# An encoder block in one kernel: the p products moved into the routing, h kept as two tensors, the last down products and the gate in halves

## The chip, the cores and the metric

The kernel runs on one core of a Trainium2 chip. The metric is the device time of one execution in microseconds, lower is better; a state of the kernel is timed in several runs and the median is compared. Times in the text are microseconds (us). The engines are named as in the profile: PE (TensorE, matmul), DVE (VectorE), ACT (ScalarE), POOL (GpSimd) and SP (SyncE, which here only issues transfers).

## What is computed

One layer of an encoder over 1024 tokens of width 1024, all in float32. What matters for the change is the second half of the layer:

```python
h = h + merged @ w_out                                     # residual after the token mixers
xn = rmsnorm(h, norm_ffn)
aff = softmax(xn @ w_router)                               # 1024 x 16
top_aff, top_idx = top_k(aff.T, 128)                       # each expert takes 128 tokens
xg = xn[top_idx]                                           # 16 x 128 x 1024
hid = silu(xg @ w_gate) * (xg @ w_up)                      # 16 experts, 1024 x 1024 each
y = (hid @ w_down) * top_aff
h = h + zeros.at[top_idx].add(y)
ple_gate = sigmoid(rmsnorm(h, norm_ple) @ w_pg)            # 1024 x 1024
h = h + ple_gate * (p @ w_ple)                             # p: 1024 x 256, w_ple: 256 x 1024
out = rmsnorm(h, norm_final)
```

## The kernel before

**Matmuls.** Every float32 product is made of three: each operand is split into a rounded high part and the rest (`split`, a CAST on ACT and a subtraction on DVE), and `mm3` (L124 for its matmuls) multiplies high by high, high by low and low by high into one bank of PSUM. Transposes are `turn` (L127). While `in_order` is set, PE runs `mm3` and `turn` in the order in which the program calls them; the other engines' order is the scheduler's, bent by `issue_after`, and the order of an engine is fixed when the program is built.

**Tile loop** (about 875 to 996 us). `w_half(t, c, between)` makes column half c of merged @ w_out for token tile t, and calls steps of the tile before at set places within its matmuls (`h_turned`, `router`, `affinities`, `aff_turned`). Its result is added into `ht` by DVE (L1194), and POOL writes `ht` to `h_d` in memory. `aff_turned` copies the turned affinities into `cand` (L1249, L1251), and after tiles 3, 5 and 6 a part of the selection's sorting follows on DVE (`four_tiles`, `two_tiles`, `merged`; MAX8 and MATCH_REPLACE, L1076 and L1078).

**Routing** (996 to 1020). After the last tile DVE finishes the sort, finds each expert's threshold (`cg`), and masks and matmuls with `tri` and `ones` give each token its place; `tokens(e)` turns places into indices by one-hot matmuls (L1345), `gather(e)` fetches the rows (`xg`) by an indirect DMA on POOL. Between these steps stand eight of the sixteen halves of p @ w_ple, `p_half(0)` to `p_half(7)`: 6 matmuls of 128x512 each, whose result ACT scales (L1173) into a slot and writes to `pw_d` in memory.

**Experts** (1020 to 1591). Each expert is 12 quarters (4 each of gate, up, down) of 1 MB of weights: `quarter_of` loads it by SP (the pieces 12 to 15 by POOL) into one of 15 buffers named by `cycle`, splits it into high and low parts (slots of `whl`, every third of `rawE`), and makes 12 matmuls of 128x512. `begin` turns an expert's rows, `hidden_turned` its hidden values; `down(e - 1)` follows `up(e)`. The down result is scaled by ACT (L1458) and added into `h_d` by one indirect scatter of 4 KB rows per expert.

**Gate** (1591 to the end). The other half of the p products (tiles 4 to 7, eight halves, in `p_product`) is made first, with the loads of p and w_ple for them; then `front(t)` turns a tile's rows of h and sums their squares, and `ple(t)` makes the gate's product with w_pg (whose rows are scaled by a gain when it is split, L982), the sigmoid by Tanh, the sum and the last norm.

## Time and profile before

| | us |
|---|---|
| median of 3 runs | 1713.43 (1713.2 to 1713.58) |
| profiled execution | 1716.04 |
| its span, first to last instruction | 1714.3 |
| PE busy | 1640.6 (96%) |
| DVE busy | 1172.4 (68%) |
| ACT busy | 904.7 (53%) |
| POOL busy | 155.4 (9%) |
| mean granted clock of PE, as a share of 2.4 GHz | 0.986 |

PE is busy nearly always, so the rows to look for are those in which it waits, and those in which its matmuls take longer than elsewhere at a lower granted clock (the two levels are 1.2 and 2.4 GHz; 0.50 in a stretch means that all of it was at the lower one). A timeline row that ends in brackets gives the idle time of the engine ahead of the row, and the instruction whose end released it.

### The profile page before, as it was taken

The numbers are of one execution on the slowest core, as the hardware profiler recorded it, in microseconds if no ns is written. First come the engines' busy times: TensorE is split into PE (matmuls) and PEld (weight loads), VectorE is DVE, ScalarE is ACT, GpSimd is POOL, SyncE is SP. The second block draws the span as 40 slices with busy tenths as digits, with TensorE's granted clock in tenths as the row PEclk, the third lists the DMA queues.
The fourth block names the chain that finished last, engine by engine and source line by source line (L and its number), as shares of the span: only waits on it lengthen the run. The fifth ranks groups of instructions, "written<-read, shape, count | busy, mean of one in ns | idle before, by whom it ended". The sixth has DMA issues, their size and how long they took to land. (4 is left out here: it accounts for less than half of the span.)

```text
span 1714.3 us, 23072 instructions
## 1 busy us (share of the span) xinstructions
PE 1640.6 (96%) x8795; PEld 1347.7 (79%) x8795; DVE 1172.4 (68%) x2228; ACT 904.7 (53%) x1273; POOL 155.4 (9%) x186
## 2 busy tenths in 40 slices
PE   7999989998999999999999959999999999999897
PEld 7978856567889898988887647888888887777786
DVE  7446655553474747473356878999999998888666
ACT  5345545542443435352033237777777777777632
POOL 1013300000000000000001110111111111100010
PEclk9999999999999999999999979999999999999999
DMA  6033421225121121126452589999999999992811
GB/s 234 2 106 123 136 61 50 62 98 173 50 65 59 56 69 43 44 75 234 147 198 111 193 333 375 382 397 388 394 391 398 394 387 370 377 380 88 275 50 50
DMA packets 123607, 335.06 MB, mean 195 GB/s; under 512 B 9180, under 2 KB 41988, under 8 KB 123496
## 3 DMA queue, kind: packets, MB, share of 16 engines
q1 hardware_dynamic: 106784, 277.96, 44.4%
q0 software_dynamic: 14704, 53.17, 9.1%
q10 hardware_dynamic: 2008, 2.46, 0.4%
q8 instruction: 69, 1.13, 0.3%
q14 instruction: 42, 0.34, 0.1%
HBM read 290.50 MB, written 43.06 MB: 195 GB/s over the span
## 5 line engine op out<-in xcount | busy, mean ns | idle before, releaser
L131 DVE TENSOR_TENSOR slot<-slot 128x2048 fp32r<-128x2048 f32 (+1 forms) x200 | 446.5, 2246 | 52.5 <-ACT slot L131 50.0
L131 ACT CAST slot<-slot 128x2048 fp32r<-128x2048 f32 (+1 forms) x200 | 374.8, 1879 | 104.2 <-PE ps_mm L124 57.0
L124 PE MATMUL ps_mm<-aT_h,wh 128*128 128x512 f32 x512 | 204.8, 400 | 0.0
L124 PE MATMUL ps_mm<-aT_l,wh 128*128 128x512 f32 x512 | 201.4, 393 | 0.0
L124 PE MATMUL ps_mm<-aT_h,wl 128*128 128x512 f32 x512 | 200.8, 392 | 0.0
L124 PE MATMUL ps_mm<-slot,xt_h 128*128 128x512 f32 x512 | 161.7, 396 | 3.1 <-DVE slot L131 2.7
L124 PE MATMUL ps_b<-slot,xt_h 128*128 128x512 f32 x512 | 160.2, 393 | 4.0 <-DVE slot L131 4.0
L124 PE MATMUL ps_mm<-slot 128*128 128x512 f32 x576 | 140.5, 398 | 0.0
L124 PEld LDWEIGHTS ps_mm<-slot 128*128 128x128 f32 x576 | 106.7, 189 | 24.2 <-issue 1.4
L124 PEld LDWEIGHTS ps_mm<-slot,xt_h 128*128 128x128 f32 x512 | 96.0, 190 | 23.7 <-DVE slot L131 3.5
L124 PEld LDWEIGHTS ps_b<-slot,xt_h 128*128 128x128 f32 x512 | 95.1, 188 | 24.7 <-DVE slot L131 5.7
L124 PEld LDWEIGHTS ps_mm<-aT_h,wh 128*128 128x128 f32 x512 | 96.6, 189 | 22.6 <-issue 6.2
L124 PEld LDWEIGHTS ps_mm<-aT_h,wl 128*128 128x128 f32 x512 | 96.6, 189 | 18.6
L124 PEld LDWEIGHTS ps_mm<-aT_l,wh 128*128 128x128 f32 x512 | 96.7, 189 | 16.4
L131 DVE TENSOR_TENSOR wl<-raw,wh 128x2048 fp32r<-128x2048 f32 (+1 forms) x29 | 60.9, 2105 | 60.9 <-ACT wh L131 60.9
L124 PE MATMUL ps_mm<-slot,xt_l 128*128 128x512 f32 x256 | 100.6, 393 | 0.6 <-DVE xt_l L131 0.6
L124 PE MATMUL ps_b<-slot,xt_l 128*128 128x512 f32 x256 | 99.8, 390 | 0.0
L131 ACT CAST wh<-raw 128x2048 fp32r<-128x2048 f32 (+1 forms) x30 | 51.9, 1734 | 82.0 <-PE ps_mm L124 78.2
L124 PE MATMUL ps_mm<-wh,aT_h 128*128 128x256 f32 x320 | 90.5, 283 | 0.0
L124 PE MATMUL ps_mm<-wl,aT_h 128*128 128x256 f32 x320 | 89.5, 280 | 0.0
L124 PE MATMUL ps_mm<-wh,aT_l 128*128 128x256 f32 x320 | 89.2, 279 | 0.0
L124 PE MATMUL ps_mm<-slot,nT_h 128*128 128x512 f32 (+1 forms) x272 | 81.9, 382 | 0.4 <-ACT nT_h L131 0.4
(386 smaller groups left out, 3281.8 us busy)
## 6 DMA issues: line engine op xcount, KB each, us to landing
slot<-in_w_exp_gate_dram SPq DMA_DIRECT2D x64, 1024.0 KB, 7.8
slot<-in_w_exp_down_dram SPq DMA_DIRECT2D x64, 1024.0 KB, 8.4
slot<-in_w_exp_up_dram SPq DMA_DIRECT2D x60, 1024.0 KB, 7.9
raw<-in_w_in_dram SPq DMA_DIRECT2D x16, 1024.0 KB, 6.6
raw<-in_w_in_dram SPq DMA_DIRECT2D x14, 512.0 KB, 5.2
sg_d<-sgr POOLq DMA_DIRECT2D x14, 512.0 KB, 2.9
xn_d<-xa POOLq DMA_DIRECT2D x8, 520.5 KB, 3.3
xt<-in_x_dram SPq DMA_DIRECT2D x8, 512.0 KB, 6.8
```

What stands on the lines that cost most here:

```text
L124: return on_pe(nc.tensor.matmul(*args, **kw))
L131: return nc.scalar.copy(hi, src), eng.tensor_sub(lo, src, hi)
```

## The change

Seven things are changed together.

1. All sixteen halves of p @ w_ple are made within the last tile's routing: one ahead of `h_turned(7)`, then one behind it, one behind the router, two behind the affinities, six behind `aff_turned`, one behind the turns of `cg`, two behind the `ones` matmuls, and two behind `tokens(0)`, whose own matmuls now stand in PE's program order. Both loads of p and the one of w_ple come at tile 3, the turns of p at tiles 4 and 5. The results of halves 8 to 15 stay in slots of `rawE` until they are written to `pw_d`.
2. `aff_turned(7)` makes its four copies on DVE (two were on ACT).
3. `four_tiles()` is called in the second half product of tile 4, behind its add, not behind `aff_turned(3)`.
4. `h_d` is two tensors, for the low and the high 512 columns, and each expert's result goes out in two scatters of 2 KB rows.
5. The down products of experts 13, 14 and 15 are made by column halves (`down_half`): the low half of 13 between gate and up of expert 15, then low 14, low 15, high 13, high 14, high 15. From expert 14 on the ring of weight buffers is 10 long.
6. w_pg is loaded into free buffers ahead of its split, and the low-half rows of tiles 0 to 3 are fetched while the high halves run.
7. The gate of tiles 0 to 2 starts with the inner blocks 0 to 3 (the low columns of h) of all three, in six banks; then the high columns are turned and the rest follows.

```diff
-    h_d = dram.tile([T, D], F32, name="h_d")
+    h_d = [dram.tile([T, 512], F32, name=x) for x in ("h_lo", "h_hi")]
...
         for g in range(2):
-            pt = bank("tr")
+            pt = bank("b")
...
+            with tc.issue_after(made):
+                four_tiles()
+        nc.gpsimd.dma_start(h_d[c][tt], ht[:, cc])
         if c == 1:
-            nc.gpsimd.dma_start(h_d[tt], ht)
             ss = small.tile([128, 1], F32, name="ss")
             junk = o2.tile([128, D], BF16, name="junk", bufs=1)
...
             to, by = cand[t][(group[t] + q) * 32:(group[t] + q) * 32 + NE], pa[0:NE, q * n:q * n + n]
-            if q % 2 and t == NT - 1:
-                nc.vector.tensor_copy(to, by)
+            if t == NT - 1:
+                placed = nc.vector.tensor_copy(to, by).ins
...
-        if t == 3:
-            four_tiles()
-        elif t == 5:
+        if t == 5:
             two_tiles()
         elif t == 6:
             merged(top[0:NE], one_tile(6), slice(0, NE), top)
...
-            p_raw = p_load(slot(rawX, (2, 4, 256))[:, 0], 0)
+        if t == 3:
+            p_raw = slot(rawX, (2, 4, 256))
+            for i in range(2):
+                p_load(p_raw[:, i], 4 * i)
             wp = parts(loaded(rawX, (2, D), w_ple), (2, D), (rawC, rawC))
-        if t == 5:
-            pT = slot(rawC, (2, 4, 2, 128), F32R)
-            p_turned(p_raw, pT)
+        elif t in (4, 5):
+            pTs.append(slot(rawC, (2, 4, 2, 128), F32R))
+            p_turned(p_raw[:, t - 4], pTs[-1])
 
 
     def p_half(n):
         nonlocal pw
         i, c = n // 2, n % 2
         if n % 4 == 0:
-            pw = slot(rawX, (2, D))
-        p_product(pw, pT, wp, i, (c,))
+            pw = slot(rawX if n < 8 else rawE, (2, D))
+        cc = slice(c * 512, c * 512 + 512)
+        pT = pTs[i // 4]
+        po = bank("mm" if c else "b")
+        for k in range(2):
+            mm3(po, pT[:, 0, i % 4, k], pT[:, 1, i % 4, k], wp[0][:, k, cc], wp[1][:, k, cc], k == 0, k == 1)
+        nc.scalar.mul(pw[:, i % 2, cc], po, 0.5)
         if n % 4 == 3:
             nc.scalar.dma_start(pw_d[(i - 1) * 128:(i + 1) * 128].rearrange("(c p) n -> p c n", p=128), pw)
 
     pw = None
     p_half(0)
-    for f, more in ((h_turned, (1,)), (router, (2,)), (affinities, (3, 4)), (aff_turned, (5, 6, 7))):
+    for f, more in ((h_turned, (1,)), (router, (2,)), (affinities, (3, 4)), (aff_turned, range(5, 11))):
         f(NT - 1)
         for n in more:
             p_half(n)
...
+    p_half(11)
     thr = o1.tile([128, 2, NE], F32, name="thr")
     nc.vector.tensor_copy(thr, pt[:, 0:2 * NE].rearrange("p (i e) -> p i e", i=2))
...
     pr = pr[:, 0:256].rearrange("p (a t e) -> p a t e", a=2, t=NT)
     sl0 = o1.tile([128, NT, NE], F32, name="sl0")
...
-            nc.tensor.matmul(pi[:, 0:2], oh[:, t], tok[:, t], start=t == 0, stop=t == NT - 1)
+            (nc.tensor.matmul if e else matmul)(pi[:, 0:2], oh[:, t], tok[:, t], start=t == 0, stop=t == NT - 1)
...
-
+    p_half(14)
+    p_half(15)
...
+    def scatter(e, c):
+        nc.gpsimd.indirect_dma_start(out=h_d[c][:, :], in_=st[e]["y"][:, c * 512:c * 512 + 512], in_offset=None,
+                                     compute_op=ALU.add,
+                                     out_offset=bass.IndirectOffsetOnAxis(ap=st[e]["idx"][:, 0:1], axis=0))
+
+    def down_half(e, c, po, after=()):
+
+        s = st[e]
+        cc = slice(c * 512, c * 512 + 512)
+        for k2 in range(2):
+            n = n_pieces[0]
+            raw = loaded(next_pool(), (4, 512), w_ed[e][k2 * 512:k2 * 512 + 512, cc])
+            hi, lo = [slot(rawE if n % 3 == 2 else whl, (4, 512), F32R) for _ in range(2)]
+            split(hi, lo, raw)
+            for k in range(4):
+                kk = 4 * k2 + k
+                mm3(po, s["hT"][0][:, kk], s["hT"][1][:, kk], hi[:, k], lo[:, k], kk == 0, kk == KC - 1)
+            for f in after if k2 == 0 else ():
+                f()
+        nc.scalar.mul(s["y"][:, cc], po, s["col"][:, e:e + 1])
+        scatter(e, c)
+
     def hidden_turned(e):
...
-        last = {1: partial(hidden_turned, e)} if e == NE - 1 else {}
         gate(e, {1: partial(hidden_turned, e - 1)} if e else {0: first_tokens})
-        up(e, {1: partial(tokens_of, e + 2)} if e else {2: partial(ahead, 1)})
-        if e:
-            down(e - 1, {0: partial(ahead, e + 1), **last})
-    down(NE - 1, {})
-
-    in_order[0] = False
-
-
...
-    cycle, n_pieces = [rawC] * 4 + [rawX] * 2 + [wraw] * 2 + [rawE] * 2 + [rawB] * 2 + [rawD], [0]
-    pws = {}
-    p_raw = p_load(next_slot((2, 4, 256))[:, 0], 4)
-    wp = parts(loaded(next_pool(), (2, D), w_ple), (2, D), (next_pool(), next_pool()))
-    pT = next_slot((2, 4, 2, 128), F32R)
-    p_turned(p_raw, pT)
-    wg = {(k, 0): mpiece(w_pg, 4 * k, 0, next_pool(), LL, gain=plcol) for k in range(2)}
-    for i in range(4):
-        if i % 2 == 0:
-            pw = next_slot((2, D))
-        p_product(pw, pT, wp, i)
-        pws[4 + i] = pw[:, i % 2]
...
+        if e == NE - 2:
+            cycle = [rawA] * 3 + [rawX] * 2 + [wraw] * 2 + [rawB] * 2 + [rawA]
+        if e == NE - 1:
+            st[NE - 3]["y"] = e2.tile([128, D], F32, name="y")
+            down_half(NE - 3, 0, bank("a"))
+        up(e, {1: partial(tokens_of, e + 2), 2: partial(ahead, NE - 1 if e == NE - 2 else NE)} if e else
+           {2: partial(ahead, 1)})
+        if 0 < e < NE - 2:
+            down(e - 1, {0: partial(ahead, e + 1)})
...
+    def first_turn(t):
+        nT = slot(whl, (2, KC, 128), F32R)
+        nTs[t] = nT[:, 0], nT[:, 1]
+        return turned_half(hs_[t], nTs[t], 0)
...
+    for c in range(2):
+        for i, e in enumerate(ends):
+            if c or i:
+                down_half(e, c, bank("b" if i % 2 else "mm"),
+                          (partial(hidden_turned, NE - 1), first_rows) if c == 0 and i == 1 else ())
+        if c == 0:
+
+            for t, rp in ((0, rawD), (2, rawC)):
+                r = lo_rows[t] = rp.tile([128, 2, D], F32, tag="raw", name="raw")
+                hs_.update({t: r[:, 0], t + 1: r[:, 1]})
+    wg, pws = {}, {}
+    raws = {}
+    for k in range(2):
+        for c in range(2):
+            raws[k, c] = loaded(rawX if k else rawC, (4, 512), w_pg[k * 512:k * 512 + 512, c * 512:c * 512 + 512])
+
+    def gate_parts(k):
+        for c in range(2):
+            pl = AA if c else (wraw if k else rawB,) * 2
+            wg[k, c] = mpiece(w_pg, 4 * k, 512 * c, None, pl, gain=plcol, raw=raws[k, c])
+
+    gate_parts(0)
+    with tc.issue_after(last_load[0]):
+        for t in (0, 2):
+            rows(lo_rows[t], h_d, t, (0,))
+        for t in range(3):
+            here = first_turn(t)
+        with ExitStack() as es:
+            for i in here:
+                es.enter_context(tc.issue_after(i.ins))
+            gate_parts(1)
+        sE.close()
+        f2 = ctx.enter_context(pool("f2", bufs=2, side="right"))
+        nfin = slot(whl, (2, D))[:, 0]
+        nc.sync.dma_start(nfin, bcast_row(norm_final, D))
+        for t in (0, 2):
+            rows(lo_rows[t], h_d, t, (1,))
+        for t in range(0, NT, 2):
+            if t > 3:
+                r = rawC.tile([128, 2, D], F32, tag="raw", name="raw")
+                rows(r, h_d, t)
+                hs_.update({t: r[:, 0], t + 1: r[:, 1]})
+            r = slot(rawX if t < 3 else rawE, (2, D))
+            nc.sync.dma_start(r, pw_d[t * 128:(t + 2) * 128].rearrange("(c p) n -> p c n", p=128))
+            pws.update({t: r[:, 0], t + 1: r[:, 1]})
+    F = {}
...
+        if t not in nTs:
+            nTs[t] = hl_pair(f2, "nT")
+            turned_half(ht, nTs[t], 0)
+        here = turned_half(ht, nTs[t], 1)[0].ins
...
+        with tc.issue_after(here):
+            nc.scalar.activation(junk, ht, AF.Square, accum_out=ss)
...
-    front(0)
-    front(1)
+    begun = {}
+    for t, tag in enumerate(("b", "mm", "a")):
+        begun[t] = [bank(tag) for _ in range(2)]
+        for po, (c0, n) in zip(begun[t], columns(t)):
+            product(po, t, c0, n, range(4))
+    for t in range(3):
+        front(t)
     for t in range(NT):
-        if t + 2 < NT:
+        ple(t, begun.get(t))
+        if t < 2:
+            front(t + 3)
+        elif 2 < t < NT - 2:
             front(t + 2)
-        ple(t)
```

**PE in the routing.** Of before, from the last turn of affinities (`affA`) to the first `tri` matmul; rows of 128x512 into `ps_b` are p products (six to a half):

```order
L127 MATMUL ps_a<-ident,affA 16x128
L124 MATMUL ps_b<-slot 128x512 x18
L127 MATMUL ps_a<-ident,cg 128x16 x2
L124 LDWEIGHTS tri
L124 MATMUL ps_a<-msk,tri 128x256
```

Of after, the same place:

```order
L127 MATMUL ps_a<-ident,affA 16x128
L124 MATMUL ps_mm<-slot 128x512 x6
L124 MATMUL ps_b<-slot 128x512 x6
L124 MATMUL ps_mm<-slot 128x512 x6
L124 MATMUL ps_b<-slot 128x512 x6
L124 MATMUL ps_mm<-slot 128x512 x6
L124 MATMUL ps_b<-slot 128x512 x6
L127 MATMUL ps_a<-ident,cg 128x16 x2
L124 MATMUL ps_mm<-slot 128x512 x6
L124 LDWEIGHTS tri
L124 MATMUL ps_a<-msk,tri 128x256
```

Six halves stand between the turn of `affA` and that of `cg` where three were, and one more ahead of `tri`.

**DVE at tile 4.** Of before, from the last affinities of tile 3 (`affA`) over the sort's last step to the second half's add (`ht`) of tile 4:

```order
L1238 TENSOR_SCALAR affA<-affA,rd_8992 128x16
L1076 MAX part<-cand_8470 128x8 x2
L1078 MATCH_REPLACE cand_8470<-part,cand_8470 128x64 x2
...
L1076 MAX part<-cand_8470 128x8 x2
L1194 SCALAR_TENSOR_TENSOR ht<-ps_mm,ht 128x512
L1100 TENSOR_TENSOR b_8475<-part 128x64
```

Of after:

```order
L1234 TENSOR_SCALAR affA<-affA,rd_8999 128x16
L1187 SCALAR_TENSOR_TENSOR ht<-ps_mm,ht 128x512
L1077 MAX part<-cand_8471 128x8 x2
L1079 MATCH_REPLACE cand_8471<-part,cand_8471 128x64 x2
...
L1077 MAX part<-cand_8471 128x8 x2
L144 TENSOR_SCALAR rs_v_9113<-ss 128x1
L131 TENSOR_TENSOR slot<-ps_b,slot 128x512
```

The add of `ht` now precedes the list of MAX and MATCH_REPLACE.

**ACT at the end.** Of before, from the last y (the down product's result) on; `slot<-ps_b` of L1173 are p products, `slot<-slot,cols` of L982 is the split of w_pg, and the CAST of `ps_tr` the first turned rows:

```order
L1458 ACTIVATE y<-ps_b,col 128x512 x2
L131 CAST slot<-ps_tr 128x512 x2
L1173 ACTIVATE slot<-ps_b 128x512 x3
L982 ACTIVATE slot<-slot,cols 128x512 x8
L1173 ACTIVATE slot<-ps_b 128x512 x4
L1547 ACTIVATE junk,ssf<-raw 128x1024
L1173 ACTIVATE slot<-ps_b 128x512
L131 CAST nT_h<-ps_tr 128x512 x2
```

Of after, the column halves of y being named `xg` and `hid` for the tiles that they reuse, and the split of w_pg L983:

```order
L1472 ACTIVATE xg<-ps_b,col 128x512
L983 ACTIVATE slot<-slot,cols 128x512 x5
L1472 ACTIVATE hid<-ps_mm,col 128x512
L983 ACTIVATE slot<-slot,cols 128x512 x3
L131 CAST slot<-ps_tr 128x512 x3
L983 ACTIVATE slot<-slot,cols 128x512 x8
L131 CAST slot<-ps_tr 128x512
L1611 ACTIVATE junk,ssf<-raw 128x1024
```

The p multiplies are gone, and five and three multiplies of w_pg stand ahead of the CAST of the first turned rows, with the last y between them.

## Rows read from the trace of the kernel before

**Rows 1.** The page, parts 1 (busy us, share, instructions) and 5 (busy us, mean ns).

```profile
PE 1640.6 (96%) x8795; PEld 1347.7 (79%) x8795; DVE 1172.4 (68%) x2228; ACT 904.7 (53%) x1273; POOL 155.4 (9%) x186
...
L131 DVE TENSOR_TENSOR slot<-slot 128x2048 fp32r<-128x2048 f32 (+1 forms) x200 | 446.5, 2246 | 52.5 <-ACT slot L131 50.0
```

**Rows 2.** Stretches: window, length, busy us by engine, PE clock, DMA share, GB/s.

```profile
1010.00:1020.00 10.00, 0.64 (x10) 0.59 (x11) 7.60 (x8) 0.00 (x0) 4.99 (x4) 0.50 0.46 157
1020.00:1030.00 10.00, 10.00 (x49) 7.78 (x48) 6.52 (x6) 3.41 (x5) 1.96 (x2) 0.70 1.02 408
1060.00:1500.00 440.00, 436.55 (x2108) 360.33 (x2107) 400.83 (x251) 341.09 (x264) 59.76 (x25) 1.00 1.02 387
```

**Rows 3.** Timeline of PE, tile 4: start, length, instruction, [idle before <- releaser].

```profile
943.14 0.66 PE L127 MATMUL ps_tr<-ident,ht 128*128 128x128 f32 x4 [2.68 <-DVE ht L1194]
943.55 3.76 PE L124 MATMUL ps_mm<-slot 128*128 128x512 f32 x9
```

**Rows 4.** Timeline of DVE, the same stretch.

```profile
937.58 0.35 DVE L1076 MAX8 part<-cand 128x8 f32<-128x64 f32 x2 [2.87 <-ACT cand L1251]
...
942.41 0.67 DVE L1194 SCALAR_TENSOR_TENSOR ht<-ps_mm,ht 128x512 f32<-128x512 f32 x1
```

**Rows 5.** Timeline of PE in the routing behind the last tile.

```profile
996.16 4.38 PE L124 MATMUL ps_b<-slot 128*128 128x512 f32 x18
1006.66 0.26 PE L127 MATMUL ps_a<-ident,cg 16*128 16x16 f32 x1 [6.12 <-DVE cg L1306]
...
1008.38 0.37 PE L124 MATMUL ps_a<-msk,tri 128*128 128x256 bf16 x1 [0.91 <-DVE msk L1318]
...
1012.00 0.38 PE L1345 MATMUL ps_a<-tok,oh 128*128 128x2 bf16 x8 [2.50 <-DVE oh L1341]
1019.74 1.94 PE L127 MATMUL ps_a<-ident,xg 128*128 128x128 f32 x8 [7.36 <-DMA xg<-xn_d,idxs]
```

**Rows 6.** Timeline of DVE, start of the last tile's sort.

```profile
996.94 0.18 DVE L1249 COPY cand<-ps_a 16x32 f32<-16x32 f32 x1 [0.29 <-ACT cand L1251]
998.67 0.18 DVE L1249 COPY cand<-ps_a 16x32 f32<-16x32 f32 x1 [1.55 <-ACT cand L1251]
```

**Rows 7.** Waits of PE, 1420 to 1592: us, times, longest us.

```profile
PE ps_b L124 <- DVE slot L131: 3.4, 3, 1.3
PE ps_mm L124 <- DVE slot L131: 2.7, 2, 1.3
PE ps_b L124 <- DVE hT_l L131: 0.8, 1, 0.8
PE ps_b L124 <- ACT hT_h L131: 0.4, 1, 0.4
```

**Rows 8.** Timeline of PE behind the last down product.

```profile
1591.43 1.03 PE L127 MATMUL ps_tr<-ident,slot 128*128 128x128 f32 x8
1592.85 7.18 PE L124 MATMUL ps_b<-slot 128*128 128x512 f32 x30 [0.38 <-ACT slot L131]
1603.36 5.72 PE L124 MATMUL ps_b<-slot 128*128 128x512 f32 x18 [3.34 <-ACT slot L1173]
...
1610.40 0.73 PE L124 MATMUL ps_mm<-slot,nT_h 128*128 128x512 f32 x2 [0.44 <-ACT nT_h L131]
```

**Rows 9.** Timeline of ACT, the same stretch.

```profile
1597.84 5.00 ACT L982 ACTIVATE slot<-slot,cols 128x512 fp32r<-128x512 f32 x8
```

**Rows 10.** Transfers: 1100 to 1400 (two rows).

```profile
DMA packets 30774, 118.36 MB, mean 395 GB/s; under 512 B 1938, under 2 KB 1938, under 8 KB 30757
...
q0 software_dynamic: 2448, 8.99, 11.0%
```

**Rows 11.** Waits of SP's queue, 1100 to 1400.

```profile
SPq L971 <- DVE slot L131: 235.5, 95, 3.2
```

**Rows 12.** Loads issued 960 to 1060: KB, median us to landing.

```profile
slot<-in_w_exp_up_dram POOLq DMA_DIRECT2D x4, 1024.0 KB, 10.1
```

**Rows 13.** Scatters: the last one; then all traffic of h_d, to landing.

```profile
h_d<-y,idxs POOLq DMA_INDIRECT x1, 6.4
...
DMA to landing us min/median/max: 2.8/10.4/13.6
```

More of the change, by code (lines that the diff above doesn't have):

```diff
@@ L1508, in tile_hybrid_block @@
-    hs_ = {}
-    def rows(src, t, n=2):
-        r = next_pool().tile([128, 2, D], F32, tag="raw", name="raw")
-        return r, nc.sync.dma_start(r[:, 0:n], src[t * 128:(t + n) * 128].rearrange("(c p) n -> p c n", p=128)).ins
-    def keep(d, t, n, r):
-        d.update({t + i: r[:, i] for i in range(n)})
-    r, first = rows(h_d, 0, 1)
-    keep(hs_, 0, 1, r)
-    with tc.issue_after(first):
-        wg.update({(k, 1): mpiece(w_pg, 4 * k, 512, next_pool(), AA, gain=plcol) for k in range(2)})
-        keep(pws, 0, 2, rows(pw_d, 0)[0])
-        keep(hs_, 1, 2, rows(h_d, 1)[0])
-        nfin = next_pool().tile([128, 2, D], F32, tag="raw", name="raw")[:, 0]
-        nc.sync.dma_start(nfin, bcast_row(norm_final, D))
-        for t in (2, 4, 6):
-            keep(hs_, t + 1, 2 if t < 6 else 1, rows(h_d, t + 1, 2 if t < 6 else 1)[0])
-            if t == 2:
-                keep(pws, t, 2, rows(pw_d, t)[0])
@@ new lines, in rows, with first_rows @@
+    def rows(r, src, t, halves=range(2)):
+        for c in halves:
+            nc.sync.dma_start(r[:, :, c * 512:c * 512 + 512],
+                              src[c][t * 128:(t + 2) * 128].rearrange("(c p) n -> p c n", p=128))
+    ends = range(NE - 3, NE)
+    hs_, nTs = {}, {}
+    def first_rows():
+        st[NE - 1]["y"] = e2.tile([128, D], F32, name="hid")
+    def first_turn(t):
+        nT = slot(whl, (2, KC, 128), F32R)
+        nTs[t] = nT[:, 0], nT[:, 1]
+        return turned_half(hs_[t], nTs[t], 0)
@@ L1572, in ple @@
         sm = small.tile([128, 1], F32, name="ssm")
[L1573 removed]
+        nc.vector.tensor_reduce(sm, ss[:, 0:len(columns(t))], axis=X, op=ALU.add)
         rs = rstd_of(sm, D)
```

81 lines of the change are left out of this document (39 added, 42 removed).

## The prediction

> **What bounds the kernel now.** I read the engine totals first: TensorE is busy for 1640.6 us of a span of 1714.3 [rows 1], so a gain must take matmul time off the path, fill an idle stretch, or raise the clock in one. Next the stretches [rows 2]: in the 440 us of the experts PE is busy for 436.6 at a clock of 1.00, so almost nothing is to be had there. In 1010 to 1020 (routing's end) it is busy for 0.64 us of 10 at a clock of 0.50. Then I went through PE's and DVE's rows where the diff touches them: the sorting beside tile 4 [rows 3, 4], the routing tail [rows 5, 6], the late experts [rows 7] and the stretch between the last expert and the first gate product [rows 8, 9]; last, what the DMA queues have in hand [rows 10 to 13].
>
> The profiled execution took 1716.04 us with a span of 1714.3; the median of three is 1713.43. I sum changes against the span and subtract the sum from the median, as though the launch costs the same.
>
> **The p products leave the end.** Between the end of the last down product (1591.43) and the first gate product (1610.40) lie 18.97 us [rows 8]: 8 turns of p (1.03), 48 matmuls of eight halves (7.18 + 5.72), waits of 0.38, 3.34 and 0.44, and the first front's turns. The 48 cost 0.239 us each in the first row (7.18/30) and 0.318 in the second (5.72/18), so the second ran partly at half clock after the 3.34 us of idle: 18 at the first rate would be 4.3. All of this goes; the p products' work moves into gaps of the routing (below). In its place, PE turns four blocks for each of tiles 0 to 2 and waits for ACT and DVE. ACT's new order puts the last y product's multiply, which waits for the last matmul, ahead of three gate multiplies and the CAST of the turned rows. An ACT operation on 128x512 takes 5.00/8 = 0.63 us [rows 9]; four multiplies and the CAST, 3.1 us, then a DVE subtraction of the same size, 3.7, and two or three hand-overs of 0.38 as in [rows 8]: 4.5 us. 18.97 less 4.5 is 14.5 gained. Against it I set 0.4 for a hand-over at the second half turns of tiles 0 to 2, which now stand in a row ahead of the rest of the gate, and 1.0 for a lower clock after the new idle (the 18 matmuls above lost 1.4 after 3.34 us of it). The 72 matmuls on low column halves (72 x 0.239 = 17.2 us) cover the last high-half scatter and its rows: multiply 0.6, scatter and landing 6.4 to 10.4 [rows 13], and for 0.5 MB pieces of rows about half of the 10.1 us of 1 MB [rows 12]; 12 to 16 us. **End: -13.1, bounds -17 (nothing lost in clock or hand-overs, turned rows ready at once) to -9 (the rows late, or a dip as long as the one at 1603).**
>
> **Routing.** Eight halves in place of those that ran there before (halves 1 to 7, and one turn of p is in the tile loop already) come into the gaps. What is on the path is DVE's: the copy of the second candidates waited 1.55 us for ACT's, which stood behind p multiplies, so the sort began behind it, after 998.85, where the matmuls behind the affinities' turn had begun at 996.16 [rows 5, 6]. All four copies on DVE remove that wait and the 0.29 ahead of the first, and add two copies of 0.18: -1.5. In PE's order half 11 now precedes the tri matmul: the gap there is 0.91 us [rows 5], the half 1.46 (6 x 4.38/18): +0.55. Halves 12 and 13 precede the one-hot matmuls, whose gap is 2.50 [rows 5]; two halves cost 2.9: +0.3 to +0.4. Halves 14 and 15 follow those matmuls, where PE waits 7.36 us for the gathered rows: hidden. So the gather starts about 0.8 earlier. Halves 5 to 10 (8.8 us) replace 18 matmuls (4.38) and fill most of the 6.12 us wait for cg: 4.4 us more against 6.1, hidden with 1.7 to spare, at full clock.
>
> **The experts' start** has a gain and a loss. PE ran at half clock there: the granted clock is 0.50 for 1010 to 1020 and 0.70 for 1020 to 1030 [rows 2]. With p halves in the gaps I expect the clock to be held to about 1014 and the idle before the gather to be some 4 to 5 us, not 7; of the 3 us that a clock of 0.70 costs in those 10 I count somewhat under half as saved: -1.3. The loss: the third quarter's hi and lo parts go to slots of rawE, which hold p rows 8 to 15 until these are written out. They are multiplied last (half 15 at about 1014), and 1 MB transfers among the expert loads there took 10.1 us to land [rows 12], so the last is out about 1025 to 1027; DVE's subtraction for that quarter (2246 ns in the mean [rows 1]) starts then and the next quarter's stands behind it. PE would want that quarter about 1026 and gets it about 1029. Some of this is met by the pieces behind it being prepared at 2.25 against some 2.8 for PE's 12 matmuls (0.239 each [rows 8]): +2.8 less 0.5. Net with the earlier gather (-0.8) and clock (-1.3) it is about **+0.2, and with the copies' reserve not all turned into time I take +0.5; bounds -2.5 (dip gone, p rows out early) to +4.5 (dip kept, p rows 3 us later).**
>
> **The tile loop.** The sort of four tiles (4.83 us of DVE, 937.58 to 942.41) stood ahead of tile 4's second residual add, and PE waited 2.68 us for it, then ran 9 matmuls in 3.76 us where the rate of [rows 8] makes 2.2 of them [rows 3, 4]. The change puts it behind that add: 2.68 + 1.6 gained there. But DVE then idles from 937.58 to about 940, when that product is ready to be added, and does the same list 2.4 us later. Tile 4's norm and affinities stand behind that list on DVE and come 2.4 us later, while PE gets to their turn some 4 us sooner than before: the wait comes back one step on. I count it even. One turn of p more in the loop is up to 1.03 [rows 8]; the split into two h tensors costs POOL eight more issues, off the path. **+0.8, bounds -2 to +2.5.**
>
> **The late experts.** PE waited 3.4 + 2.7 us for DVE's slots and 1.2 for hT between 1420 and 1592 [rows 7]: experts 12 to 15, whose ACT order alternates CAST and hid multiply, lose the longest, 1.3, each. In the new order two of the four (12 and 15) have CAST, CAST, hid, hid: 2 x 1.3 gone; the last down product's hT (0.4 + 0.8) is now turned a whole product earlier: 1.2 gone; 0.4 back for smaller pieces. **-3.4, bounds -5.5 to +1** (the ring of raw buffers shrinks from 15 to 10 from expert 14 on, and a wait for a load would be new). All 16 scatters become two halves each; POOL was busy for 155.4 us in all [rows 1] and can take 16 scatters more.
>
> **Sum:** -13.1 + 0.5 + 0.8 - 3.4 = -15.2. With 1713.43: 1698.2, rounded to **1698.5**, since hand-overs that I have not seen are likelier to add than to take away.
>
> A rule of the Trainium skill speaks to the halves: "DMA: Bandwidth & Descriptors", Rules for kernel authors, says that an accumulating transfer beside another access of the same bytes must wait for the earlier one's semaphore, since the accumulate reads and later writes its destination. The kernel keeps it, since each scatter waits for the last into its tensor; no run here shows what happens without. The same page's Specifications put one core's share of the memory at about 358 GB/s; the row at 1100 to 1400 shows 395 [rows 10], so the measurement decides; by 358 the 118.36 MB would have taken 331 us instead of 300, and the sum would be lost to the transfers.
>
> **Rivals.** *(a) All hidden:* no clock dip after the experts, the tile loop keeps the 2.68 and p rows are out in time: -1.0 - 3.5 - 1.3 on the sum, **1692.5**. For it: the rows at full rate wherever PE has no gap before them. Against: ACT's order at the end fixes a gap. *(b) Routing pays:* the p rows 8 to 15 land after 1029 or the clock stays at half through the p halves, so that they delay the sort's end: 3.5 to 5 us over my sum, **1703**. For it: 10.1 us to land [rows 12], loads queued beside it. *(c) The chain of low-half scatters:* those of experts 13, 14, 15 go out in turn, 5.5 us apart for the last two, and each waits for the one ahead; one lands in 6.4 us with queues empty, and the median over all of h_d's traffic is 10.4 [rows 13]. At 6.4 tile 0's rows are in SBUF some 4 us before the last matmul, at 10.4 about 4 us after it: 3 to 5 us over the sum, **1702**. *(d) Slower, the transfers become the bound:* the experts' loads already run at 395 GB/s, with q0's scatters and gathers at 11.0% of the engines' time [rows 10]. Half rows make 128 packets more per expert; at the 0.216 engine-us that q0's packets take (11.0% of 300 x 16 over 2448) they cost up to 1.7 us of 35 per expert, 27 over sixteen. That decides only if the queue has no slack: SP waited 235 of 300 us for DVE to free a buffer [rows 11], and fifteen buffers of 1 MB are 15/12 of an expert's 35 us ((1591.4 - 1019.7)/16), of which a load takes about 10 to land: some 30 us of lead. It has to use up the 15 us of gain and that lead, 2.8 us per expert. Then it gives **1715 to 1720**. *(e) The change does not do what it says*, that is, the gaps in routing are not filled because p's multiplies (0.6 each, sixteen) hold up ACT's affinities: the p products cost there what they did at the end, 10 of their 12.9 us come back: **1708**.
>
> **How the numbers follow.** My forecast 0.48, (a) 0.12, (b) 0.16, (c) 0.14, (d) 0.04, (e) 0.06. The bounds of the four terms, taken together as independent (4, 3.5, 2.3, 3.3), are about 6.5 us, so the forecast's own range is 1692 to 1705; it takes in (a), (b) and (c). I set 1690.5 to 1705.5; (d), (e) and the outer ends of (b) and (c) are left out. A measurement of this kernel can tell about 0.2%, 3.4 us: faster is under 1710, slower over 1716.9. (d) is split between same and slower, a quarter of (e) is same, and 0.01 of slower is for what I have not seen: faster 0.94, same 0.03, slower 0.03.
>
> **What would show it.** In the changed profile: no multiply of p between the experts and the gate, and about 3 us of PE idle there; the first sort of the last tile within 1 us of the affinities' turn; a DVE subtraction at the experts' start that waits for a pw_d transfer; no PE wait for ht in tile 4, but one for affA; two waits of 1.3 us fewer in the late experts; the experts' total PE time the same. I am wrong if waits for raw loads (ACT waiting for DMA) appear in the experts, if the gate starts more than 7 us after the last down product, or if the routing stretch grows.

## The result

The changed kernel takes **1697.58 us** (median of 4 runs, 1696.55 to 1699.41) against 1713.51 for the kernel before in the same runs: a ratio of 0.9908, with a 95% interval of 0.9896 to 0.9919. Forecast were 1698.5 us and 1690.5 to 1705.5. The size was right; the sum behind it was not right in every term, and that errors of several microseconds in both directions cancelled was luck.

The page of the changed kernel, part 1 (busy us, share of the span, instructions), which answers to [rows 1]:

```profile
PE 1634.3 (96%) x8795; PEld 1345.4 (79%) x8795; DVE 1169.3 (69%) x2229; ACT 902.7 (53%) x1270; POOL 201.0 (12%) x210
```

DVE's mean for the weight subtraction (2245 ns) and the number of matmuls (8795) are unchanged. The span is 18.4 us shorter in the two profiled executions (1714.3, 1695.9), 15.9 in the medians; the profiled execution of before was 2.5 us over its own median.

**Where the time went.** I cut both timelines at the same instructions of PE and POOL: S, the first matmul of the tile loop; C, the turn of the thresholds `cg`; G, the issue of expert 0's gather; X, the turn of the gathered rows; T, the end of the last down product (the start of the turn behind it, less its wait); P, the first gate product; E, the end of the span. The rows of the changed kernel, PE's timeline (start, length, instruction, idle time ahead of it and what ended it), which answer to [rows 3, 5, 8]:

```profile
874.74 9.46 PE L124 MATMUL ps_mm<-slot 128*128 128x512 f32 x41
...
952.53 0.27 PE L127 MATMUL ps_a<-ident,affA 128*16 128x128 f32 x1 [2.28 <-DVE affA L1234]
...
993.55 0.27 PE L127 MATMUL ps_a<-ident,affA 128*16 128x128 f32 x1 [0.88 <-DVE affA L1234]
...
1000.51 1.52 PE L124 MATMUL ps_b<-slot 128*128 128x512 f32 x6
1002.54 0.20 PE L127 MATMUL ps_a<-ident,cg 16*128 16x16 f32 x1 [0.50 <-DVE cg L1307]
...
1020.23 1.94 PE L127 MATMUL ps_a<-ident,xg 128*128 128x128 f32 x8 [8.88 <-DMA xg<-xn_d,idxs]
...
1587.95 1.06 PE L127 MATMUL ps_tr<-ident,raw 128*128 128x128 f32 x8 [0.50 <-DMA raw<-h_lo]
1591.55 0.66 PE L127 MATMUL ps_tr<-ident,raw 128*128 128x128 f32 x4 [2.54 <-DVE slot L131]
1591.97 5.73 PE L124 MATMUL ps_b<-slot 128*128 128x512 f32 x24
...
1610.42 0.66 PE L127 MATMUL ps_tr<-ident,raw 128*128 128x128 f32 x4 [0.97 <-DVE slot L131]
```

Of the kernel before, only S is not among the rows above:

```profile
875.38 9.00 PE L124 MATMUL ps_mm<-slot 128*128 128x512 f32 x39
```

POOL's gather, of before and then of after:

```profile
1012.93 2.82 POOL L1353 DMA_INDIRECT xg<-xn_d,idxs  x1 [15.78 <-DVE idxs L1347]
```

```profile
1009.02 2.84 POOL L1357 DMA_INDIRECT xg<-xn_d,idxs  x1 [14.45 <-DVE idxs L1351]
```

| stage (us) | before | after | moved | by the prediction |
|---|---|---|---|---|
| S to the last affinities' turn (996.14, 993.55) | 120.76 | 118.81 | -1.95 | +0.8 |
| affinities' turn to C | 10.52 | 8.99 | -1.53 | -1.5 |
| C to G | 6.27 | 6.48 | +0.21 | +0.9 |
| G to X | 6.81 | 11.21 | +4.40 | 0 |
| X to T | 571.69 | 567.22 | -4.47 | -3.4, and +1 at the start |
| T to P | 18.97 | 4.52 | -14.45 | -14.5 |
| P to E | 103.90 | 103.93 | +0.03 | +1.4 |

S itself came 0.64 earlier, in a part that the change doesn't touch. Together that is 18.4.

**The stretches** that answer to [rows 2] (columns as there):

```profile
1010.00:1020.00 10.00, 1.36 (x6) 0.76 (x5) 4.27 (x3) 3.60 (x4) 4.78 (x5) 0.81 0.76 267
1020.00:1030.00 10.00, 9.36 (x45) 7.18 (x46) 5.59 (x6) 3.19 (x4) 1.02 (x1) 0.68 1.03 420
1060.00:1500.00 440.00, 438.12 (x2116) 361.84 (x2115) 402.54 (x254) 343.20 (x265) 87.23 (x37) 1.00 1.01 381
```

PE is busy for 1.36 us of 1010 to 1020, and 1020 to 1030 ran at 0.68. Behind the gathered rows the half clock lasts as long as it did, 5.8 us (1020.23 to about 1026.0, before 1019.74 to about 1025.5); ahead of them, from C to G, the clock is now full (1.00 in 1002.50 to 1005.40), where it was at 0.50 (1006.60 to 1009.50). What PE waited for in the experts, 1060 to 1580 (us, times, longest), against [rows 7]:

```profile
PE ps_mm L124 <- DVE slot L131: 1.9, 2, 1.3
PE ps_b L124 <- DVE slot L131: 1.3, 1, 1.3
```

3.2 us where there were 7.3. The transfers of 1100 to 1400 that answer to [rows 10, 11]: q0's packets, and SP's wait for buffers:

```profile
q0 software_dynamic: 3561, 8.90, 11.5%
```

```profile
SPq L971 <- DVE slot L131: 235.5, 95, 3.2
```

There are 1113 packets more, but the share rose from 11.0% to 11.5% only, and SP waits for DVE exactly as long as before. So over the experts the transfers were no nearer to being the bound.

**The gather.** It is issued 3.9 us earlier (1009.02 against 1012.93), and its rows are turned 0.5 us later (1020.23 against 1019.74): the whole gain of tile loop and sort is gone by X. The queues between 1008 and 1021 in the changed kernel (packets, MB, share), and what was issued (KB each, median us to landing):

```profile
q1 hardware_dynamic: 441, 1.74, 39.7%
q10 hardware_dynamic: 266, 1.02, 19.5%
q0 software_dynamic: 195, 0.74, 15.3%
...
slot<-in_w_exp_up_dram POOLq DMA_DIRECT2D x4, 1024.0 KB, 24.2
slot<-in_w_exp_gate_dram SPq DMA_DIRECT2D x2, 1024.0 KB
pw_d<-slot ACTq DMA_DIRECT2D x1, 1024.0 KB
slot<-in_w_exp_down_dram SPq DMA_DIRECT2D x1, 1024.0 KB
xg<-xn_d,idxs POOLq DMA_INDIRECT x1, 11.1
```

In the kernel before, the same stretch behind the gather's issue (1012 to 1021) has q0 alone:

```profile
q0 software_dynamic: 395, 1.54, 50.1%
...
slot<-in_w_exp_up_dram POOLq DMA_DIRECT2D x3, 1024.0 KB, 9.2
xg<-xn_d,idxs POOLq DMA_INDIRECT x1, 6.7
```

Two weight loads of SP (at 1011.2 and 1011.6, into buffers that the p products held until half 15), the last write of p products (ACT, 1012.02) and a third load of SP (1014.30) now run beside the gather:

```profile
1011.16 0.88 SPq L971 DMA_DIRECT2D slot<-in_w_exp_gate_dram  x2
1014.30 0.37 SPq L971 DMA_DIRECT2D slot<-in_w_exp_down_dram  x1
```

Whether they are the cause is what four of the experiments ask.

### The profile page after: what moved, and what is told of

Read it like the earlier page. It is cut to its first block, busy times and chain, and to the rows that moved or that the text cites. A ratio compares the mean times of both kernels' runs of the same rounds, so it can differ in the third digit from the quotient of the medians.

```text
span 1695.9 us, 23146 instructions
## 1 busy us (share of the span) xinstructions
PE 1634.3 (96%) x8795; PEld 1345.4 (79%) x8795; DVE 1169.3 (69%) x2229; ACT 902.7 (53%) x1270; POOL 201.0 (12%) x210
## 5 line engine op out<-in xcount | busy, mean ns | idle before, releaser
L131 DVE TENSOR_TENSOR slot<-slot 128x2048 fp32r<-128x2048 f32 (+1 forms) x200 | 446.2, 2245 | 51.3 <-ACT slot L131 46.7
L124 PE MATMUL ps_mm<-slot 128*128 128x512 f32 x720 | 174.5, 395 | 0.0
L124 PEld LDWEIGHTS ps_mm<-slot 128*128 128x128 f32 x720 | 132.4, 188 | 29.1 <-issue 1.4
L124 PE MATMUL ps_b<-slot,xt_h 128*128 128x512 f32 x480 | 149.8, 392 | 1.9 <-DVE slot L131 1.9
L124 PEld LDWEIGHTS ps_b<-slot,xt_h 128*128 128x128 f32 x480 | 89.1, 188 | 20.5 <-DVE slot L131 2.7
L124 PE MATMUL ps_b<-slot,xt_l 128*128 128x512 f32 x240 | 93.6, 390 | 0.0
L124 PE MATMUL ps_b<-slot 128*128 128x512 f32 x384 | 92.4, 392 | 0.1
```

Source lines behind the costliest of these rows:

```text
L124: return on_pe(nc.tensor.matmul(*args, **kw))
L131: return nc.scalar.copy(hi, src), eng.tensor_sub(lo, src, hi)
```

## The experiments

The executions of one kernel differ by up to 8 us within a group of runs (1710.89 to 1718.96 for the kernel before, 1695.13 to 1701.97 for the changed one), more than most single edits are worth. A part of that arises ahead of the tile loop (S lies between 874.4 and 877.9) and in its clock: S to C is 127.5 to 129.4 us for the same code. So beside each median stand the stages of the profiled execution, cut as above. All ratios are to the kernel before in the same group of runs; only those of gate_whole and of the last two runs lie outside what the three intervals of the unaltered changed kernel span (0.9883 to 0.9934), so the single edits rest on the stages of one execution each.

| run | S to C | G to X | X to T | T to P | P to E | median | ratio (95%) |
|---|---|---|---|---|---|---|---|
| before | 131.3 | 6.8 | 571.7 | 19.0 | 103.9 | 1713.51 | |
| after | 127.8 | 11.2 | 567.2 | 4.5 | 103.9 | 1697.58 | 0.9908 (0.9896 to 0.9919) |
| after_again | 127.5 | 11.7 | 566.5 | 4.6 | 103.9 | 1700.21 | 0.9921 (0.9907 to 0.9934) |
| sort_ahead | 128.5 | 11.5 | 565.8 | 4.5 | 103.9 | 1699.23 | 0.9915 (0.9901 to 0.9928) |
| copies_act | 129.2 | 11.3 | 566.3 | 4.4 | 103.9 | 1698.87 | 0.9918 (0.9904 to 0.9932) |
| p8_no_matmul | 127.4 | 6.3 | 567.9 | 4.9 | 105.0 | 1697.82 | 0.9905 (0.9891 to 0.9918) |
| quiet_gather2 | 129.2 | 6.3 | 569.9 | 4.8 | 105.2 | 1699.10 | 0.9904 (0.9890 to 0.9919) |
| y_behind_gate | 127.7 | 11.5 | 566.6 | 2.9 | 103.9 | 1696.56 | 0.9893 (0.9879 to 0.9908) |
| silu_behind | 129.0 | 11.3 | 562.8 | 4.9 | 105.0 | 1697.22 | 0.9896 (0.9881 to 0.9910) |
| gate_whole | 129.1 | 11.4 | 566.4 | 16.9 | 102.6 | 1708.89 | 0.9966 (0.9955 to 0.9978) |
| late_write_only | 127.8 | 9.5 | 570.1 | 4.6 | 105.3 | 1700.20 (1 run) | |
| after_third | 129.4 | 11.4 | 566.5 | 4.9 | 106.4 | 1698.39 | 0.9899 (0.9883 to 0.9916) |
| all_three | 129.2 | 6.6 | 565.3 | 3.0 | 104.0 | 1690.04 | 0.9852 (0.9835 to 0.9869) |
| all_three_bank | 127.9 | 6.3 | 565.7 | 2.2 | 103.9 | 1689.02 | 0.9853 (0.9837 to 0.9870) |

### The changed kernel again (after_again, after_third)

No edit. 

> The changed kernel once more, unaltered, as the yardstick of this group on the same chip. Both theories: 1697.6 us, within 1.5 us; 15.9 us under the kernel before.

 And beside the last group: 

> The changed kernel unaltered, as the yardstick beside the two that follow. Both theories: 1697 to 1700 us.

 Measured: 1700.21 and 1698.39, the first 2.6 us above what was expected. Against the kernel before in their own groups (1713.56, 1714.92) that is 13.4 and 16.5 us less. Their gathers land 11.7 and 11.4 us behind the issue, as in the first profile (11.2), so that delay is no accident of one execution.

### The sort ahead of the add (sort_ahead)

```diff
-        if c == 1 and t == 4:
-            with tc.issue_after(made):
-                four_tiles()
...
+        if t == 3:
+            four_tiles()
+        elif t == 5:
```

> One part undone: the sort of four tiles is called behind the affinities of tile 3 again, ahead of the add of tile 4's second half. Theory from the two traces: the affinities' turn of the last tile came 2.6 us earlier after the change, although one turn of p (0.8 us) was added to the loop, so the new place of the sort is worth 2.5 to 3.5 us: this run is 2.5 to 3.5 us slower than the changed kernel, with the 2.7 us wait of PE for ht back and matmuls behind it at half clock. Rival, the reading of the prediction: the wait only moves one step on to the affinities, and the time is the same within 0.5 us.

 Measured: S to C 128.5 against 127.5 and 127.8 of the unaltered kernel; the median can't tell it from the unaltered kernel (1700.21). PE's wait for `ht` is back, at 1.8 us, but the matmuls behind it kept their clock:

```profile
942.86 0.66 PE L127 MATMUL ps_tr<-ident,ht 128*128 128x128 f32 x4 [1.82 <-DVE ht L1187]
943.27 2.32 PE L124 MATMUL ps_mm<-slot 128*128 128x512 f32 x9
...
953.51 0.27 PE L127 MATMUL ps_a<-ident,affA 128*16 128x128 f32 x1 [0.84 <-DVE affA L1231]
```

and the wait for the affinities is 0.84 where the changed kernel has 2.28. From S to the turn of tile 5's affinities this run takes 90.03 us (875.11 to 965.14), the changed kernel 89.43 (874.74 to 964.17), both with all matmuls at full clock: the new place is worth 0.6 us. (Behind that, 15 matmuls of this run take 5.26 us where the changed kernel needs 3.67, so the 0.7 to 1 us of S to C are not the edit's alone.) So the wait does mostly move one step on, as the prediction had it; the 2.5 to 3.5 us of the theory are far off, and the rival's 0.5 is just missed. The largest part of the 1.95 us in the loop, 1.45, is half clock behind that wait in the profiled execution of before (3.76 us for 9 matmuls, [rows 3], against 2.31).

### Two copies on ACT again (copies_act)

```diff
-            if t == NT - 1:
-                placed = nc.vector.tensor_copy(to, by).ins
+            if q % 2 and t == NT - 1:
+                nc.vector.tensor_copy(to, by)
```

> One part undone: two of the four candidate copies of the last tile are on ACT again, behind multiplies of p. Theory of the prediction: the last sort starts 1.5 us later, so the gather is issued 1.5 us later and the time is 1.5 us longer. Rival: the gathered rows land when the transfers beside them (weight loads and the last write of p products) let them, at about 1020 us whatever the sort does, and the time is the same within 0.5 us.

 Measured: from the same S (874.63 and 874.61), the thresholds' turn comes at 1003.81 against 1002.15, 1.66 us later, and the gathered rows at 1021.62 against 1020.30, 1.3 later; the span is 1.0 longer. From the affinities' turn to C it is 10.49 us against 9.00. The medians (1698.87 and 1700.21) don't show it. The step of the prediction holds (1.5), and the landing is no fixed time: what comes earlier at the gather's issue does come earlier at its landing.

### No matmuls for halves 8 to 15 (p8_no_matmul)

```diff
-        po = bank("mm" if c else "b")
-        for k in range(2):
-            mm3(po, pT[:, 0, i % 4, k], ...)
+        if n < 8:
+            ...
+        else:
+            po = wp[0].rearrange("p a b -> p (a b)")[:, cc].bitcast(F32)
```

> The 48 matmuls of the p products' halves 8 to 15 are left out (ACT scales columns of the split w_ple in their place, so p @ w_ple is wrong for tiles 4 to 7); their multiplies, slots and writes stay. Theory: in the routing those matmuls lie beside DVE's sort and the wait for the gathered rows, only halves 11 to 13 touch the path (0.4 to 0.8 us): this run is 0 to 1 us faster. Rival one: they are on the path as they were at the end, 48 x 0.228 = 10.9 us, and at least 3 us come off. Rival two: they keep PE's clock up, and without them the routing and the first expert run at half clock: 1 to 3 us slower.

 Measured: S to C (127.4 us) is that of the unaltered kernel, and C to G is 6.20 us against 6.48 with these matmuls in, so they cost 0.3 us there and lie beside other work otherwise. But the gathered rows come 5.3 us earlier, 6.3 us behind the issue. With the multiplies free of matmuls, both writes of these rows are issued at 885 and 893, in the tile loop, and the two weight loads at 997.8, ahead of the gather, and SP's next load comes at 1019.75; of the traffic of these queues only the tail of a write was still in flight at the gather's issue (20 to 60 GB/s until 1009.8). In this execution the first gate products lose 1 us to half clock (P to E 105.0), as in four other runs. No statement foresaw the gather: the matmuls cost next to nothing, the transfers that wait for them did.

### The gather alone (quiet_gather2)

```diff
-            nc.scalar.dma_start(pw_d[...], pw)
+            with tc.issue_after(gathered) if n == 15 else ExitStack():
+                (nc.gpsimd if n == 15 else nc.scalar).dma_start(pw_d[...], pw)
...
+        if behind is not None:
+            nc.vector.tensor_copy(raw[:, 0, 0:1], behind[:, 0:1])
```

(`behind` is the gathered rows' tile, for weight pieces 10 and 11.) 

> The changed kernel with the first gather kept alone: the last write of p products (rows 1536 on of the second half, 1 MB) is issued by POOL behind the gather, and the two weight loads that SP issued at 1011 wait for the gathered rows (a one-column copy by DVE out of these rows into their buffers). Theory: the rows landed 11.7 us after the gather's issue, against 6.8 in the kernel before and 6.3 where the matmuls of halves 8 to 15 were left out, because of these transfers; alone they land in 6.3 to 7 us, at 1015.5 instead of 1020.3, and 4 to 5 us come off the experts' start, of which late waits may take back 1: 1695 to 1697 by the yardstick's 1700.2. Rival: the landing depends on what was in flight before the gather, or on the gather's own queue, and it stays at 11 us, with the time the same within 1 us.

 Measured: landing at 6.3 us, as expected. PE's row of the gathered rows, and the row that follows where the third quarter's split was late:

```profile
1019.88 1.36 PE L127 MATMUL ps_a<-ident,xg 128*128 128x128 f32 x8 [3.99 <-DMA xg<-xn_d,idxs]
...
1029.87 0.50 PE L124 MATMUL ps_mm<-slot,xt_h 128*128 128x512 f32 x1 [0.80 <-DVE slot L131]
```

About 5 us come off G to X, and 3.3 of them go again in X to T (569.9 against 566.5): the scheduler had put ACT's CASTs and silu passes of the late experts back into the alternating order, and the waits for DVE slots are 6.0 us again (3.3 into `ps_b`, 2.7 into `ps_mm`). The median, 1699.10, is above the 1695 to 1697 expected.

### Only the write behind the gather (late_write_only)

The first half of that diff alone. 

> The changed kernel with one of the two repairs of the run with the gather alone: the last write of p products is issued by POOL behind the gather, while the two weight loads of SP stay where the change put them, 2.1 and 2.6 us behind the gather's issue. If the write is what slows the gather, its rows land 6.3 to 7 us behind the issue, as when it was alone; if the two loads (2 MB) are, they land 10 to 11.5 us behind it; if each takes its share, 8 to 9.5 us.

 Measured: issue at 1008.98, rows turned at 1018.45, 9.5 us. So the two loads cost the gather some 3.1 us (9.5 less 6.3). The other 2 are not the write's alone: the third load, which SP issues at 1014.30 in the changed kernel, comes only at 1028.55 here, behind the gathered rows. The write and the third load cost 2 us together, and no run parts them. X to T shows that moving this one write is enough to turn ACT's order in the late experts back: the waits for DVE slots are 6.0 us here too.

### The last y behind the gate's multiplies (y_behind_gate)

```diff
+        with tc.issue_after(ahead_of_y()) if ahead_of_y else ExitStack():
+            nc.scalar.mul(s["y"][:, cc], po, s["col"][:, e:e + 1])
```

(`ahead_of_y` splits the first part of w_pg and returns ACT's last multiply of it.) 

> The changed kernel with one order turned: ACT makes all eight multiplies of the first part of w_pg ahead of the last y, not five ahead and three behind it. Theory of the prediction's sum: these three (1.9 us) stand between the last matmul of the experts and the first gate product, so the 4.5 us there become 2.6 to 3.0. Rival: the rows of h_lo or DVE's part of the split are later than ACT, and the 4.5 us stay.

 Measured: T to P 2.9 us, 1.6 less. ACT of the changed kernel, then of this run:

```profile
1582.64 3.16 ACT L983 ACTIVATE slot<-slot,cols 128x512 fp32r<-128x512 f32 x5
1587.49 0.69 ACT L1472 ACTIVATE hid<-ps_mm,col 128x512 f32<-128x512 f32 x1 [1.69 <-PE ps_mm L124]
1588.08 1.93 ACT L983 ACTIVATE slot<-slot,cols 128x512 fp32r<-128x512 f32 x3
1589.92 1.05 ACT L131 CAST slot<-ps_tr 128x512 fp32r<-128x512 f32 x2
```

```profile
1583.45 5.00 ACT L983 ACTIVATE slot<-slot,cols 128x512 fp32r<-128x512 f32 x8
1588.36 0.67 ACT L1473 ACTIVATE hid<-ps_mm,col 128x512 f32<-128x512 f32 x1
1589.37 1.08 ACT L131 CAST slot<-ps_tr 128x512 fp32r<-128x512 f32 x2 [0.34 <-PE ps_tr L127]
```

ACT had sat idle for 1.69 us ahead of the last y with three multiplies still to do. The theory holds.

### Silu behind the second CAST (silu_behind)

```diff
+            if q == 1 and "silu" in s:
+                with tc.issue_after(lo_ins[1]):
+                    s["silu"]()
```

> The changed kernel with ACT's order in experts 13 and 14 like that of the others: both silu passes behind the second weight CAST of the up product. Theory of the prediction: the alternating order costs PE 1.3 us in each of them, so two of the three waits for DVE slots between 1420 and 1570 vanish (3.2 us in all become 0.5 to 0.6). Rival: the waits come from the shorter ring of weight buffers, and stay.

 Measured: the waits of 1060 to 1580 are

```profile
PE ps_mm L124 <- DVE slot L131: 0.5, 1, 0.5
```

and X to T is 562.8, 3.7 less than in after_again, of which 2.7 are these waits; where the other 1.0 comes from was not followed up. The ring of buffers is as short as in the changed kernel, so the rival falls.

### The gate not begun with the low columns (gate_whole)

```diff
-    for t, tag in enumerate(("b", "mm", "a")):
-        begun[t] = [bank(tag) for _ in range(2)]
-        for po, (c0, n) in zip(begun[t], columns(t)):
-            product(po, t, c0, n, range(4))
```

> One part undone: the gate's products of tiles 0 to 2 are not begun with the low columns; every product runs whole, behind the turns of both halves. The column halves of the last down products stay. Theory: PE then waits from the last matmul of the experts for the last high-half scatter and its rows, 0.7 + 6.4 + 4 or more, so the first product starts 12 to 15 us behind the last down product instead of 4.5, and the time is 7 to 11 us longer. Rival: the scatter and the rows are quicker with empty queues, and the loss is under 4 us.

 Measured: 1708.89 us, ratio 0.9966 (0.9955 to 0.9978). PE's rows behind the last down product:

```profile
1602.86 1.94 PE L127 MATMUL ps_tr<-ident,raw 128*128 128x128 f32 x8 [8.93 <-DMA raw<-h_hi]
...
1606.12 6.08 PE L124 MATMUL ps_mm<-slot 128*128 128x512 f32 x20
```

The first product starts 16.9 us behind the last down product, not 4.5 and later than the 12 to 15 expected, and the time is 8.7 to 10.5 us over the unaltered kernel (1700.21, 1698.39; other groups of runs). So most of the gain at the end needs this part: taking the p products away alone would have left a wait for the last scatter in their place.

### The repairs together (all_three, all_three_bank)

The diffs of the three runs above, silu for experts 1 to 14; then, for the bank:

```diff
-        return turned_half(hs_[t], nTs[t], 0)
+        return turned_half(hs_[t], nTs[t], 0, "a" if t == 2 else "tr")
```

> The changed kernel with three repairs together: the first gather kept alone, the eight multiplies of w_pg ahead of the last y, and both silu passes of every expert from 1 to 14 behind the second CAST of the up product. Theory, from the stages of the three single runs: 5.3 us at the gather (landing 6.3 us behind its issue), 1.6 to 1.9 at the gate, 2.7 to 3.7 in the late experts now that the waits which the earlier gather turned into are gone too; 8 to 11 us together: 1687 to 1691. Rival: what the gather gives back is taken again by waits for DVE slots, as in the run with the gather alone (6.0 us of them against 3.2), and under 6 us remain.

 

> The same with the first turn of tile 2 into one of the banks that the last down products of expert 13 left, not into a bank that tile 0's turned rows must leave first. Theory: PE's wait of 0.96 us ahead of tile 2's turn goes and the first product waits for tile 0's split instead; the gate starts 0.3 to 0.9 us sooner. Rival: the first product needs that split anyway, and the start is the same within 0.2 us.

 Measured: 1690.04 and 1689.02 us, ratios 0.9852 and 0.9853 to the kernel before, against 0.9899 of the changed kernel in the same group: 0.46% or some 8 to 9 us faster than it, and 25 faster than the kernel before. The waits of the late experts are 1.6 us, T to P is 3.0 and 2.2. The bank brings 0.7 us at that place, which the medians don't show. Of the gather's 5 us the experts' start takes some 1.3 back: PE now waits for DVE at the quarter whose split stands behind the write of p rows,

```profile
1015.13 1.06 PE L127 MATMUL ps_a<-ident,xg 128*128 128x128 f32 x8 [3.98 <-DMA xg<-xn_d,idxs]
...
1026.32 0.50 PE L124 MATMUL ps_mm<-slot,xt_h 128*128 128x512 f32 x1 [1.67 <-DVE slot L131]
```

a wait that the later rows and the half clock behind them had hidden in the changed kernel: there the first turns of the rows take 1.94 us behind 8.88 us of idle, here 1.06 behind 3.98.

## Why the prediction was right

**The end, right.** T to P was forecast as 18.97 less 4.5, and is 4.52. P to E is the same 103.9 as before, so the two additions did not show in it. The hand-over at the second half turns (0.4) was there and larger, 0.97 us at 1610.42, but four turns fewer than before stand behind P and a wait of 0.28 us behind the first products is gone. The dip of the clock (1.0) did not come in this execution. It does occur: of the twelve profiled executions that begin the gate so, seven run the first 24 matmuls in 5.7 us and five in 6.8 to 8.2, the longest in after_third.

```profile
1593.92 8.19 PE L124 MATMUL ps_b<-slot 128*128 128x512 f32 x24
```

**The sort, right.** -1.5 forecast, -1.53 measured, and copies_act gives 1.49 back in that stage. Halves 11 to 13 cost 0.2 in place of 0.9, as C to G shows. Half 11 does delay `tri` by about the 0.55 forecast (C to `tri` 2.18 us against 1.72), but the 14 `ones` matmuls behind it take 0.61 us instead of 0.97, now that the clock is full there; the sum took them at their old rate. One slip of the sum: its terms for the routing (-1.5, +0.55, +0.35) make the gather 0.6 us earlier, not the 0.8 that it carries on.

**The late experts, right in kind.** 7.3 us of waits became 3.2 (-4.1, forecast -3.4): I had counted 0.4 for the smaller pieces, which cost nothing, and one short wait shrank from 0.8 to 0.5.

**The gather, wrong.** The step that failed is "Halves 14 and 15 follow those matmuls, where PE waits 7.36 us for the gathered rows: hidden." The matmuls are hidden: PE waits 8.88 us behind them, and still 3.99 in quiet_gather2, where the rows come early. What the step left out are the transfers that wait for these halves: the buffers that they free (two loads of 1 MB) and the rows that they finish (one write of 1 MB) start within 3.0 us of the gather's issue, about as long as POOL's own instruction takes (2.84 us), a third load follows, and the gathered rows are turned 11.2 to 11.7 us behind the issue instead of 6.3 to 6.8. With that one of the prediction's own signs of being wrong came true: the routing stretch grew, from 23.60 us (996.14 to 1019.74) to 26.68 (993.55 to 1020.23). I had looked at that write only for the slot it holds. In the kernel before the DMA engines were busy for less than half of that time (0.46 of 1010 to 1020, [rows 2]), which was the sign. The Trainium skill has the rule ("DMA: Bandwidth & Descriptors", Issuing engines are not separate DMA queues): transfers started by SP, ACT and POOL run on the same 16 engines and interleave whoever started them. The runs agree: 6.3 us with none of these transfers beside it, 9.5 beside two loads, 11.2 to 11.7 beside three loads and the write.

**The experts' start, wrong twice.** The wait for p rows 8 to 15 is there on DVE:

```profile
1025.79 2.29 DVE L131 TENSOR_TENSOR slot<-slot 128x2048 fp32r<-128x2048 f32 x1 [2.27 <-DMA pw_d<-slot]
```

at 1025.79, within the 1025 to 1027 of the forecast, but PE lost 0.4 us there, not 2.3, because the gathered rows were late, it ran at half clock until about 1026 and so came late itself; and the half clock, of which I had expected 1.3 us back, stayed: PE was idle for 8.9 us ahead of the gathered rows, not for 4 to 5. The two errors offset each other (1.9 less lost, 1.3 less gained). Routing and experts' start together were forecast as +0.5 and came out at about +2.7 (-1.53 + 0.21 + 4.40 - 0.37, the last being X to T less the late waits).

**The tile loop, wrong.** +0.8 forecast, -1.95 measured. That the wait moves on was right (2.28 us for the affinities in place of 2.68 for `ht`). The step that failed is "I count it even", which sets a returning wait against all of the 2.68 + 1.6 gained. It let DVE idle to about 940 and begin the list 2.4 us later; the product was ready to be added at 937.3, and the list began 0.37 us later than before (1.0 counted from S):

```profile
937.34 0.69 DVE L1187 SCALAR_TENSOR_TENSOR ht<-ps_mm,ht 128x512 f32<-128x512 f32 x1 [3.28 <-PE ps_mm L124]
937.95 0.34 DVE L1077 MAX8 part<-cand 128x8 f32<-128x64 f32 x2
```

And the 1.6 us of half clock behind the old wait (3.76 us for 9 matmuls) did not come again behind the new one in this execution. They are not sure to be won: with the old order sort_ahead ran the same 9 matmuls in 2.32 us, and with the new one after_third met half clock behind the wait for the affinities (a granted clock of 0.65 in 953.50 to 958.40):

```profile
955.16 3.42 PE L124 MATMUL ps_mm<-slot 128*128 128x512 f32 x9
```

From S to the last affinities' turn after_third takes 120.39 us, only 0.37 less than the kernel before. So most of the -1.95 can be the execution's; between two executions at full clock the order is worth 0.6 us (sort_ahead). How often the kernel before meets the half clock stays open, since one trace of it was kept.

**The sum.** The errors are -2.75 in the loop, +2.2 in routing and start, -0.7 in the late experts, -1.3 at the end, and -0.6 ahead of the loop. In the medians the change is worth 13.4 to 16.5 us in three groups of runs, forecast 15.2: the total came out by errors that offset each other, and in part by the luck of the executions. Rival (c), the chain of low-half scatters, came within half a microsecond: PE waits 0.50 us for the rows of `h_lo` at 1587.95 (1.36 at most in the other runs). What rival (b) names did not happen: C came earlier by all that was forecast and the p halves ran at full clock. Its price, 3.5 to 5 us in the routing, was paid all the same, at the gather (+4.40). Rival (e) falls: PE's wait for `cg` is 0.50 us, where it was 6.12. Rival (d) is far off: half scatters raised q0's share by 0.5 points of 300 us, some 0.2 us of engine time per expert, not 1.7. Why S varies by 3 us from execution to execution was not followed up.

## What to carry to other kernels

Work that is moved into a gap brings its transfers along, and the buffers that it frees release the loads of others: ask what is in flight at that moment on the DMA engines, and whether a small transfer that everybody waits for (here 0.5 MB of gathered rows) is among it. A wait that disappears at one place is worth only what the next engine in the row has in hand; read the next late thing from the trace ahead of counting it. Where single edits are smaller than the spread of the runs, cut the timeline at the same instructions and compare stages.

## What the hardware showed that was not expected

An indirect gather of 128 rows of 4 KB took 6.2 to 6.7 us to land with little beside it, 9.3 beside two loads of 1 MB that were issued 2 to 3 us after it, and 11.1 beside these, a write of 1 MB and a third load. Twice the packets for the same bytes in the scatters cost far less than in proportion: q0 had 3561 packets in 300 us instead of 2448, and 11.5% of the engines' time instead of 11.0%.
